# Part of an HBM-to-HBM quadrant swap sent through SBUF, beside direct copies

## The chip, the cores and the metric

The kernel runs on one core of one Trainium2 chip; the other cores have nothing to do. The metric is the device time of one execution in microseconds. The time before is the median of three runs. The profile is of one execution and gives a span a little shorter than the timed figure.

## What is computed

The input `x` is a matrix of 8192 x 8192 float32, which is 256 MiB or 268.44 MB. The output is `np.fft.ifftshift(x)`: as both sides are even, rows are rotated by 4096 and columns by 4096, so that the four quadrants change places diagonally.

```python
def setup_inputs():
    return {"x": np.random.randn(8192, 8192).astype(np.float32)}

def reference(x):
    return np.fft.ifftshift(x)
```

Nothing is computed on the values. Every byte is read once from HBM and written once to HBM, at another place. Sizes below are in MiB where they count blocks, and in MB (10^6 bytes) where they stand beside rates.

## The kernel before

The kernel copies from HBM to HBM and never touches the on-chip memory SBUF. The list `quads` holds the four quadrants as pairs of an output region and the input region that goes there. A loop over the quadrants cuts each into `nsplit = 4` blocks of 1024 rows, and for each block line 41 issues one copy, a DMA of 1024 rows of 4096 columns, 16 MiB. There are 16 such DMAs, all issued by the sync engine (SP) in one queue, one after the other. One row of a block is 16 KiB of contiguous memory; the next row of the same block lies 32 KiB further on, for reads and for writes.

A DMA is carried out by the core's 16 DMA engines together. Each takes a sixteenth of its rows, here 64 rows, and moves each row as one packet, so that the program makes 16 x 1024 = 16384 packets of 16 KiB. [...]

The layer in which the kernel is written (Tile) puts the waits in. It hands out eight completion semaphores in turn, one to each DMA in its order of issue. A DMA that takes a semaphore again waits, on the engine that issues it, until the DMA that had it before has landed completely. In this kernel the ninth DMA so waits for the first, and so on. No copy depends on the data of another.

Of the kernel before, what the change touches and what calls it, by code (L numbers as in the profile page):

```python
# [1 line left out]

# [4 lines left out]


@with_exitstack  # L10
def kernel(
    ctx: ExitStack,
    tc: tile.TileContext,
    x: bass.AP,
    out: bass.AP,
):
    nc = tc.nc

    R, C = x.shape
    hr = R // 2  # L20
    hc = C // 2

    quads = [
        ((0, hr), (0, hc), (hr, R), (hc, C)),
        ((0, hr), (hc, C), (hr, R), (0, hc)),
        ((hr, R), (0, hc), (0, hr), (hc, C)),
        ((hr, R), (hc, C), (0, hr), (0, hc)),
    ]

    engines = [nc.sync]  # L30
    nsplit = 4
    k = 0
    for (or0, or1), (oc0, oc1), (ir0, ir1), (ic0, ic1) in quads:
        rows = or1 - or0
        step = rows // nsplit
        for s in range(nsplit):
            a = s * step
            b = a + step
            eng = engines[k % len(engines)]
            k += 1  # L40
            eng.dma_start(
                out=out[or0 + a : or0 + b, oc0:oc1],
                in_=x[ir0 + a : ir0 + b, ic0:ic1],
            )


# [1 line left out]
_INS = ['x']  # L48
_OUTS = [((8192, 8192), 'float32')]


def kernel(**inputs):
    import numpy as _np
    import concourse.bacc as _bacc
    import concourse.tile as _tile
    from concourse import mybir as _mybir
    from concourse.bass_utils import run_bass_kernel_spmd as _run

    nc = _bacc.Bacc("TRN2", target_bir_lowering=False, num_devices=1)  # L59
    arrays, args = {}, []  # L60
    for name in _INS:
        a = _np.ascontiguousarray(inputs[name])
        if a.dtype.kind in "iu":
            a = a.astype(_np.int64)
        arrays[f"in_{name}_dram"] = a
        args.append(nc.dram_tensor(f"in_{name}_dram", a.shape, _mybir.dt.from_np(a.dtype), kind="ExternalInput").ap())
    for i, (shape, dtype) in enumerate(_OUTS):
        dt = _mybir.dt.from_np(_np.dtype(dtype))
        args.append(nc.dram_tensor(f"out_{i}_dram", shape, dt, kind="ExternalOutput").ap())
    with _tile.TileContext(nc) as tc:  # L70
        kernel(tc, *args)
    r = _run(nc, [arrays], core_ids=[0])
    got = tuple(r.results[0][f"out_{i}_dram"] for i in range(len(_OUTS)))
    return got[0]
```

## Time and profile before

| what | before |
| --- | --- |
| time, median of 3 runs | 823.21 us (820.71 to 828.84) |
| span of the profiled execution | 811.5 us |
| bytes moved by the DMA engines | 268.44 MB in 16640 packets |
| mean rate of the DMA engines | 331 GB/s |
| HBM traffic, read and written | 2 x 268.44 MB, 662 GB/s over the span |
| DMA issues | 16 of 16384 KB, median 158.0 us from issue to landing |
| compute engines | idle; 4 small memsets on GpSimd, 0.2 us |

The rate of the DMA engines counts a byte once when it passes an engine, where it is read and written. For a copy from HBM to HBM the HBM's own traffic is twice that. The 256 packets beyond the 16384 are the small ones that count up the semaphores, one for each DMA on each engine. Where the profile gives a DMA share, it is the mean share of time in which the 16 DMA engines have a packet in hand, not a share of their peak rate.

### The profile page before, as it was taken

To read this page: it belongs to the slowest core of one execution; us is meant where nothing else is said; L and a number is where in the kernel's file an instruction comes from. 1 tells how busy PE (TensorE), PEld (TensorE's weight loads), DVE (VectorE), ACT (ScalarE), POOL (GpSimd) and SP (SyncE) were. 2 spreads that over 40 slices of the span, in tenths; PEclk is the share of its full clock that TensorE was granted. 3 is DMA by queue.
4 is the path that set the end of the run, shared out by engine and by line. 5 is a ranking of instruction groups with operands and counts; after the bars stand their busy time and mean duration, and the time that the engine had idled before them with its cause. 6 is when DMAs were issued, how large, how long until landed. Compare 5 with 4: busy or idle time off the path is not lost. (4 is left out here: it accounts for less than half of the span.)

```text
span 811.5 us, 61 instructions
## 1 busy us (share of the span) xinstructions
POOL 0.2 (0%) x4
## 2 busy tenths in 40 slices
POOL 0000000000000000000000000000000000000000
DMA  9999999999999999999999999999999999999998
GB/s 298 328 328 333 312 337 332 326 334 329 332 334 329 329 329 334 331 331 334 338 340 333 332 334 339 334 333 337 338 333 337 334 333 338 332 334 341 328 339 287
DMA packets 16640, 268.44 MB, mean 331 GB/s; under 512 B 256, under 2 KB 256, under 8 KB 256
## 3 DMA queue, kind: packets, MB, share of 16 engines
q1 hardware_dynamic: 16640, 268.44, 99.3%
HBM read 268.44 MB, written 268.44 MB: 662 GB/s over the span
## 5 line engine op out<-in xcount | busy, mean ns | idle before, releaser
L59 POOL MEMSET const-bfloat16-1.0<- 128x1 bf16 x1 | 0.1, 102 | 0.0
L59 POOL MEMSET const-uint8-127<- 128x1 uint8 x1 | 0.1, 101 | 0.0
L59 POOL MEMSET const-float32-0.0<- 128x1 f32 x1 | 0.1, 99 | 0.2 <-issue 0.2
L59 POOL MEMSET const-float32-1.0<- 128x1 f32 x1 | 0.1, 98 | 0.0
## 6 DMA issues: line engine op xcount, KB each, us to landing
out_dram<-in_x_dram SPq DMA_DIRECT2D x16, 16384.0 KB, 158.0
```

The lines of the kernel that those rows point to most:

```text
L59: nc = _bacc.Bacc("TRN2", target_bir_lowering=False, num_devices=1)
```

## The change

The last 1280 output rows (40 MiB) no longer go straight from HBM to HBM. They go through SBUF in pieces of 128 rows by 2048 columns (1 MiB, 8 KiB in each of the 128 partitions): one DMA loads a piece into a tile, and another stores it from there. There are 20 tiles, each with a buffer of its own, and 40 pieces, so each tile is used twice (`CYCLES = 2`). Loads and stores are issued by the scalar engine (ACT), from a queue of its own.

The other 6912 rows (216 MiB) remain direct copies on the sync engine, but in 108 DMAs of 128 rows by 4096 columns (2 MiB) rather than 16 MiB each. In the text of the kernel one direct copy follows each load and each store, and the copies left over come at the end. A DMA of 128 rows gives each engine 8 rows[...].

The idea is to let loads and stores, each of which uses HBM in one direction alone, run beside copies that use it in both.

```diff
+P = 128
+TILES = 20
+CYCLES = 2
...
+    piece = hc // 2
+    pool = ctx.enter_context(tc.tile_pool(name="bounce", bufs=1))
...
+    def src(row):
+        return (row + hr) % R
+    through = [
+        (row, col)
+        for row in range(R - P * TILES * CYCLES // 4, R, P)
+        for col in range(0, C, piece)
+    ]
+    direct = [
+        (row, col) for row in range(0, R - P * TILES * CYCLES // 4, P) for col in (0, hc)
+    ]
+    tiles = [pool.tile([P, piece], x.dtype, name=f"t{k}") for k in range(TILES)]
-    engines = [nc.sync]
-    nsplit = 4
...
-            eng.dma_start(
-                out=out[or0 + a : or0 + b, oc0:oc1],
-                in_=x[ir0 + a : ir0 + b, ic0:ic1],
+    def copy():
+        if direct:
+            row, col = direct.pop(0)
+            nc.sync.dma_start(
+                out=out[row : row + P, col : col + hc],
+                in_=x[src(row) : src(row) + P, hc - col : 2 * hc - col],
             )
+    for c in range(CYCLES):
+        for k, t in enumerate(tiles):
+            row, col = through[c * TILES + k]
+            oc = (col + hc) % C
+            nc.scalar.dma_start(out=t[:], in_=x[src(row) : src(row) + P, oc : oc + piece])
+            copy()
+        for k, t in enumerate(tiles):
+            row, col = through[c * TILES + k]
+            nc.scalar.dma_start(out=out[row : row + P, col : col + piece], in_=t[:])
+            copy()
+    while direct:
+        copy()
```

More of the change, by code (lines that the diff above doesn't have):

```diff
@@ L21 @@
     hc = C // 2
[L23 to L27, printed above, removed]
-    ]
-    engines = [nc.sync]
-    nsplit = 4
[L32 to L41, printed above, removed]
-                out=out[or0 + a : or0 + b, oc0:oc1],
-                in_=x[ir0 + a : ir0 + b, ic0:ic1],
-            )
+    piece = hc // 2
[6 more added lines that the diff above has]
+        for col in range(0, C, piece)
+    ]
+    direct = [
[8 more added lines that the diff above has]
+                in_=x[src(row) : src(row) + P, hc - col : 2 * hc - col],
+            )
+    for c in range(CYCLES):
[10 more added lines that the diff above has]
+        copy()
 _INS = ['x']
```

## The prediction

> **What bounds the kernel now.** I read the page's DMA lines first, since no compute engine has work.
>
> ```profile
> span 811.5 us, 61 instructions
> ...
> GB/s 298 328 328 333 312 337 332 326 334 329 332 334 329 329 329 334 331 331 334 338 340 333 332 334 339 334 333 337 338 333 337 334 333 338 332 334 341 328 339 287
> ...
> q1 hardware_dynamic: 16640, 268.44, 99.3%
> HBM read 268.44 MB, written 268.44 MB: 662 GB/s over the span
> ```
>
> The 16 DMA engines hold a packet during 99.3% of the span, and the rate is flat: one stage from end to end, no gaps. A 16 KiB packet takes 16 x 811.5 us x 0.993 / 16384 = 0.787 us on average. That isn't an engine's best. In the trace's packet records 34% of these packets took 608 or 611 ns, the least that occurs (26.8 GB/s an engine, 429 for 16); the median is 731, the longest 2053. So packets wait for something all engines share.
>
> Next, the direct copies by line, for whether issue is the limit, and the windows at the end, where some engines have finished (columns: length, GpSimd busy, clock, DMA share, GB/s).
>
> ```profile
> L41 SPq DMA_DIRECT2D out_dram<-in_x_dram x16: 582/49353/95664, 0.7 to 652.6; - x16
> ...
> DMA to landing us min/median/max: 53.7/158.0/199.5
> ```
>
> ```profile
> 804.00:806.00 2.00, 0.00 (x0) 1.00 1.05 344
> 806.00:807.00 1.00, 0.00 (x0) 1.00 0.91 295
> 807.00:808.00 1.00, 0.00 (x0) 1.00 0.81 279
> 808.00:809.00 1.00, 0.00 (x0) 1.00 0.68 246
> 809.00:810.00 1.00, 0.00 (x0) 1.00 0.20 82
> ```
>
> The last DMA was issued at 652.6 us, 159 us before the end: the queue is always full and issue costs nothing. At the end, rate over busy share rises from 295/0.91 = 324 through 279/0.81 = 344 and 246/0.68 = 362 to 82/0.20 = 410 GB/s (narrow windows, so rough). Fewer engines run faster each: the shared limit is HBM at some 662 GB/s of reads plus writes, with the engines' own ceiling of 429 GB/s above it.
>
> **What the Trainium skill says.** "HBM Reference", Specifications (TRN2), gives about 716 GB/s for the HBM of a pair of cores; 662 is 92% of it, so the trace agrees that little is left. "Advanced Engine Details and Errata", DMA Bandwidth Details, gives 27.2 GB/s for an engine; the best packets' 26.8 agrees. "DMA: Bandwidth & Descriptors", Issuing engines are not separate DMA queues, says DMAs from different engines share the same 16 DMA engines and interleave; the trace before has one queue and can't show it. The same page's Latency and other measured facts bears on a rival below.
>
> **The change, part by part.**
>
> Bytes. HBM still reads and writes 268.44 MB each: no HBM work is saved. The DMA engines carry the 40 MiB twice, in 40 loads and 40 stores of 1 MiB: 226.5 MB direct + 83.9 MB = 310.4 MB, 16% more. What was the slack resource is charged.
>
> Order. The text of the kernel pairs one direct copy (2 MiB) with each load or store (1 MiB). The order as built doesn't: Tile orders them load, copy, load, again and again, then store, copy, store, so there are **two loads or stores for each direct copy**: 40 groups with 80 loads or stores and 40 copies, and 68 copies alone at the end. All share the eight semaphores, so each DMA waits on its issuing engine for the one eight places before it in this common order. The copies can't run ahead of the loads: the ratio of bytes is 1 to 1, whatever the engines' arbitration gives.
>
> Waits. Behind a waiting DMA stand the later ones of its queue. Eight in flight are about 5 loads or stores and 3 copies, 11 MiB; at 407 GB/s (below) that is some 28 us of work. At the end eight copies are 16 MiB, 50 us. A copy that waits leaves the ACT queue filled, so I cost these waits at nothing. A store stands at least 20 DMAs behind its load, and the load that reuses a tile as far behind the store: both are covered by the same waits. Issues cost at most some 0.6 us (the shortest on SP is 582 ns) for 188 DMAs on two engines in 800 us: hidden under transfers in flight. The tiles use no compute engine.
>
> Mixed part, 40 groups. In one group each engine moves 16 packets of 8 KiB (two loads or stores) and 8 of 16 KiB (one copy). An unobstructed 8 KiB packet takes 307 ns in the trace (three of the start-up transfers' packets; half of 611 is 305).
> - Lower end: 16 x 0.307 + 8 x 0.611 = 9.80 us, 40 groups 392 us. HBM then carries 6 MiB = 6.29 MB a group, 642 GB/s, just under 662.
> - Upper end: the copies' packets stay at 0.787: 16 x 0.307 + 8 x 0.787 = 11.21 us, 448 us.
> - What I take: while both queues hold packets, 8 copy packets and 8 small ones draw 5 MiB from HBM; at 662 GB/s that is 7.92 us. The other 8 small packets run alone at engine speed, 2.46 us. Together 10.38; the 16 engines are not in step, which fills some of HBM's slack, so **10.3 us a group, 412 us**, or 167.8 MB at 407 GB/s.
>
> The same data before (120 MiB net, 60 times 2 MiB) took 60 x 8 x 0.787 = 378 us. Even the lower end loses 14 us; my value loses 34.
>
> Last part: 68 copies x 8 packets x 0.787 us = 428 us, taking a copy of 2 MiB to run at the rate of one of 16 MiB.
>
> Edges: 811.5 - 16384/16 x 0.787 = 6 us for start and end, kept. From span to time: 823.21 - 811.5 = 11.7 us, kept.
>
> Sum: 412 + 428 + 6 = 846 us span, **858 us time, 4.2% slower**.
>
> **The rivals.**
> - Engine-bound, no HBM obstruction in the mix (the shared limit eases as soon as a third of the packets use it in one direction only): 392 + 428 + 6 + 11.7 = 838 us, 1.8% slower. For it: 642 is below 662. Against: it is so close that every packet at its minimum is unlikely, when 66% miss it now.
> - HBM no better beside loads: 448 + 428 + 6 + 11.7 = 894 us. Or one direction is the limit: then 20 groups run at 9.80 us and the other 20, where 4 MiB go that way at 331 GB/s, take 12.7 us, 449 us in all and 895. Against both: mixed HBM traffic would then fall to about 560 GB/s with the engines partly obstructed.
> - Faster: direct copies alone speed up with the new shape. The engines then work 256 KiB apart rather than 2 MiB, and some of the obstruction may be clashes of places in HBM. If packets alone fell from the mean 0.787 to the median 0.731, the last part would take 398 us, and with the mix at its floor 392 + 398 + 6 + 11.7 = 808 us, 1.9% faster. For it: packets range from 608 to 2053 ns. The skill's section named above lists copies that slow with large power-of-two row pitches: 207 of 214 GB/s at 512 KiB and 164 at 2 MiB. With 8 rows an engine I work that out as engines 4 and 16 MiB apart; at 2 MiB apart, as before, I estimate under 3% lost. Its full rate of 214 lies far below the 331 measured here, so it is weak evidence, and against this case.
> - No change: the same gain at about half the size, near 823.
>
> **How the numbers follow.** My case 0.50 (858); engine-bound 0.17 (838); HBM no better, or one direction, 0.15 (894); faster 0.10 (808); no change 0.08 (823). Slower by over 1%: 0.50 + 0.17 + 0.15 = 0.82. The range goes from 830, a little under the engine-bound case, to 896, over the two worst; out are faster, no change and a little above, about 0.2.
>
> **What would show each step right or wrong.** The page after should show 310.4 MB in about 27,000 packets (24,064 of data and 188 x 16 for semaphores), at a mean of 310.4/846 = 367 GB/s, with the HBM line near 635. By slices the rate should be about 407 for the first half, then fall to about 334. Windows: the mix ends near 415 us; 390 means engine-bound, 450 HBM no better. If the last 68 copies take under 413 us, the term for copies alone is wrong; if the rate dips between slices or the DMA share falls under 0.95 in the mix, the waits are not free. If the first part passes 429 GB/s, the engines' ceiling is wrong, and with it the whole argument.

## The result, and the profile after

The changed kernel took 860.07 us (median of 3 runs, 858.95 to 861.73) against 823.21 us: 1.043 times before, 95% interval 1.037 to 1.049. It is slower.

The page of the changed kernel, the lines that answer to those shown of before (the GB/s line gives the DMA engines' rate in 40 equal slices of the span; q1 is the sync engine's queue, q10 the scalar engine's):

```profile
span 858.3 us, 233 instructions
...
GB/s 364 378 405 401 410 409 414 413 411 412 389 413 414 392 403 418 411 407 415 378 341 319 323 327 324 325 319 328 321 322 318 320 328 321 318 325 328 328 320 252
DMA packets 27074, 310.41 MB, mean 362 GB/s; under 512 B 3008, under 2 KB 3008, under 8 KB 3008
...
q1 hardware_dynamic: 15552, 226.50, 74.7%
q10 hardware_dynamic: 11520, 83.89, 24.6%
...
HBM read 268.44 MB, written 268.44 MB: 626 GB/s over the span
```

The engines carry 310.41 MB rather than 268.44, and HBM's traffic, the same in bytes, runs at 626 GB/s rather than 662. So HBM is worked less hard than before, while q1 and q10 together still fill 99.3% of the 16 engines' time. The rate falls halfway, from some 410 to some 323 GB/s. The windows of the two parts (columns: length, GpSimd busy, clock, DMA share, GB/s):

```profile
20.00:420.00 400.00, 0.00 (x0) 1.00 1.01 406
460.00:850.00 390.00, 0.00 (x0) 1.00 0.99 323
```

In the second part there are direct copies alone: 323 GB/s through the engines is 646 at HBM, 2% under the 662 of before. In the first, each group of two loads or stores and one copy moves 4 MiB through the engines and 6 MiB at HBM: 406 is 609 GB/s at HBM, well under that limit, and close to the 429 of the engines. So the engines bind here for the most part. In the trace's packet records the 16 KiB packets in the first 420 us take 642 ns on average and the 8 KiB packets 329, against least times of 608 and 307.

Where did the time go? In the engines' time, one group took 16 x 0.329 + 8 x 0.642 = 10.4 us, and 40 of them 416 us. The same data as direct copies, 60 of 2 MiB at the 0.796 us a packet that the timed runs of before imply (working below), are 382 us. That is 34 of the 37 us lost.

The queue of the sync engine, by what it waited for (columns: who waited, for what; us in total, times, longest us). L49 is the line of the direct copy; `t<-in_x_dram` is a load, `out_dram<-t` a store:

```profile
SPq L49 <- DMA out_dram<-in_x_dram: 335.1, 57, 6.6
SPq L49 <- DMA t<-in_x_dram: 210.4, 20, 16.6
SPq L49 <- DMA out_dram<-t: 202.2, 22, 13.4
```

In the mix, direct copies were held back by loads for 210 us and by stores for 202 us. So the engines got two loads or stores to a copy: from 20 to 420 us they started 9742 packets of 8 KiB and 5040 of 16 KiB. No DMA engine stood idle for it (share 1.01), so these waits look free. They are not: they set which kind of bytes the engines had to hand, as the experiments show.

### The profile page after: what moved, and what is told of

It reads as the page before. It is cut to its first block, busy times and chain, and to the rows that moved or that the text cites. A ratio compares the mean times of both kernels' runs of the same rounds, so it can differ in the third digit from the quotient of the medians.

```text
span 858.3 us, 233 instructions
## 1 busy us (share of the span) xinstructions
POOL 0.2 (0%) x4
## 2 busy tenths in 40 slices
DMA packets 27074, 310.41 MB, mean 362 GB/s; under 512 B 3008, under 2 KB 3008, under 8 KB 3008
## 3 DMA queue, kind: packets, MB, share of 16 engines
HBM read 268.44 MB, written 268.44 MB: 626 GB/s over the span
```

## The experiments

My theory: bytes through SBUF pass the DMA engines twice; with two loads or stores to one copy the mix needs the engines (429 GB/s at best) more than it needs HBM (some 660), so slack moves to HBM and is lost. The order as built and the eight shared semaphores keep it at that ratio. The rivals: the shape of the smaller copies costs; a second queue costs; a fixed cost of entering and leaving the SBUF part; or every byte through SBUF costs the same whatever stands beside it.

Four runs were made on another chip: the one queue in the order as built, the change again, the thinner mix, and the loads and stores on semaphores of their own. Before took 814.5 us beside these four and 824 to 825 beside the other eight, so runs are compared by their ratio to before.

### Copies of 2 MiB alone

```diff
-    nsplit = 4
+    nsplit = 32
```

> All 256 MiB as 128 direct copies of 2 MiB on one queue, nothing through SBUF. If the smaller copies ([...]eight semaphores over 16 MiB) are what makes the copies alone take 0.804 us a packet in the changed kernel: 1024 packets an engine x 0.804 + 8 = 831 us span, 1% over before. If the shape costs nothing and the loss is all in the SBUF part: 823, as before.

824.67 us, ratio 1.000 (0.998 to 1.002). The shape of the direct copies costs nothing that shows. The profile of before, then that of this run, columns as above:

```profile
20.00:800.00 780.00, 0.00 (x0) 1.00 1.00 333
20.00:800.00 780.00, 0.00 (x0) 1.00 1.00 328
```

Copies alone differ by this much from one execution to another. The 323 GB/s in the changed kernel's profile is a little lower still; the same kernel, run again below, has 328 there.

### Two queues of direct copies

```diff
-    engines = [nc.sync]
+    engines = [nc.sync, nc.scalar]
```

> The kernel before, its 16 copies issued in turn from the sync and the scalar engine. If HBM's 662 GB/s is what bounds direct copies, a second queue changes nothing: 823 within 1%. If a queue's own packets in flight are the limit, two queues come near the engines' 429 GB/s: about 630 us. If switching between two queues costs, slower than 830.

822.82 us, ratio 0.996 (0.992 to 0.999). A second queue hardly lifts the limit, and it doesn't cost. What bounds direct copies lies behind the queues.

### Loads alone, then stores alone

```diff
-    for c in range(CYCLES):
...
+    pieces = [(row, col) for row in range(0, R // 2, P) for col in range(0, C, piece)]
+    for n, (row, col) in enumerate(pieces):
+        nc.scalar.dma_start(out=tiles[n % TILES][:], in_=...)
+    for n, (row, col) in enumerate(pieces):
+        nc.scalar.dma_start(out=out[row : row + P, col : col + piece], in_=tiles[n % TILES][:])
```

> No direct copies: 128 loads of 1 MiB into the 20 tiles, then 128 stores of 1 MiB from them, 134 MB each way (half of the matrix is left out, and the stores write what the tiles last held, so the output holds other rows). If the engines' ceiling is 26.8 GB/s each: 313 us a stage at 429 GB/s, 8 KiB packets at 307 ns. If one direction of HBM is limited to the 331 GB/s that direct copies show: 405 us a stage.

641.68 us (one run). The windows inside the loads and inside the stores, columns as above:

```profile
20.00:300.00 280.00, 0.00 (x0) 1.00 1.01 422
340.00:620.00 280.00, 0.00 (x0) 1.00 1.01 422
```

Either direction runs at 422 GB/s, close to the 429 worked out from the shortest packets, and well above the 331 that each direction has in direct copies. So the limit of direct copies is not one direction of HBM but the sum of both, and the engines' own ceiling stands at some 422. Whether that sum is bounded in the HBM itself or on the way to it, no run here tells apart.

### Half and twice the bytes through SBUF

```diff
-CYCLES = 2
+CYCLES = 1
```

> The change with one round instead of two: 20 MiB through SBUF, 118 direct copies. If each byte through SBUF is charged for its second passage of the DMA engines, half the bytes cost half: 20 groups x 10.4 us + 98 copies x 6.43 + 8 = 846 us span, about 848. If the cost is a fixed one (a second queue, start and end of the SBUF part), it stays near 860.

836.88 us, ratio 1.014 (1.008 to 1.019). The window of its copies alone:

```profile
260.00:820.00 560.00, 0.00 (x0) 1.00 1.00 331
```

```diff
-CYCLES = 2
+CYCLES = 4
```

> The change with four rounds: 80 MiB through SBUF, 88 direct copies. Charged by bytes: 80 groups x 10.4 us + 8 copies x 6.43 + 8 = 891 us span, about 893. A fixed cost: near 860. If stores and loads of neighbouring rounds blocked each other, over 910.

879.39 us, ratio 1.064 (1.060 to 1.068). With four rounds the mix lasts nearly to the end, and its window shows the rate of the changed kernel's first part again:

```profile
20.00:800.00 780.00, 0.00 (x0) 1.00 1.01 409
```

The loss grows with the bytes, so it is no fixed cost. Both losses are smaller than I expected: 12.5 us for 20 groups and 55 for 80, or 0.6 to 0.7 us a group, where the changed kernel loses 0.9 (0.8 when run again below). The time of copies alone may explain part of this: 331 GB/s in the one-round profile, 323 in that of the change. The loss per group is known no better than that.

### One queue, in the order of the text

```diff
-            nc.sync.dma_start(
+            tc.keep_in_program_order(nc.sync.dma_start(
...
-            nc.scalar.dma_start(out=t[:], in_=...)
+            tc.keep_in_program_order(nc.sync.dma_start(out=t[:], in_=...))
...
```

The stores are changed as the loads are. `keep_in_program_order` makes Tile keep a DMA where the text has it.

> The change's DMAs, all from the sync engine in the order of its text: one load or store, then one direct copy, so that bytes through SBUF and direct bytes stand 1 to 2 in the mix; 28 copies are left alone. If the mix of the change is bound by the engines because it has too few direct bytes beside the loads and stores, this one is bound by HBM again: a group (5 MiB of HBM traffic) takes 5.24 MB / 662 GB/s = 7.92 us, 80 groups 634, 28 copies x 6.43 = 180, with edges 8 and 2: 824 us, near before. If only the bytes through SBUF count, whatever stands beside them: near 860. If packets of one queue cannot overlap each other as those of two can: over 860.

834.32 us, ratio 1.009 (1.006 to 1.012). The same 40 MiB go through SBUF as in the change, but 80 copies stand beside them and not 40, and four fifths of the loss are gone. The window of its mix:

```profile
20.00:630.00 610.00, 0.00 (x0) 1.00 1.01 389
```

A group is now one load or store and one copy, 3 MiB through the engines and 5 at HBM: 389 is 648 GB/s at HBM. The engines have slack against their 422, HBM has next to none.

### One queue, in the order as built

```diff
-            copy()
+            if n % 2 == 0:
+                copy()
+            n += 1
```

> All from the sync engine, in the order that the changed kernel has as built: two loads or stores to one direct copy. It differs from the changed kernel in the number of queues alone, and from the run with one queue in text order in the ratio alone. If the ratio in the mix is what costs: as the changed kernel, about 855. If the second queue is what costs: about 834, as the run with one queue in text order.

842.64 us, ratio 1.034 (1.031 to 1.038). It differs from the run above in the ratio alone (this edit, after each load and each store), and from the changed kernel in the number of queues alone.

```profile
20.00:380.00 360.00, 0.00 (x0) 1.00 1.01 420
440.00:830.00 390.00, 0.00 (x0) 1.00 1.00 327
```

In its mix the engines reach 420 GB/s, their ceiling in loads and stores alone, and HBM stands at 420 x 1.5 = 630. The ratio makes most of the loss, with one queue as with two: 1.034 at two to one against 1.009 at one to one, with the same bytes through SBUF.

### The change again

The changed kernel without an edit, on the other chip.

> The changed kernel once more, beside the next three, so that all four stand against the same runs of before. Expected: 1.043 times before, about 860; if the first measurement lay high, 1.03, which would put it on the line through one round (1.0137) and four rounds (1.0642).

847.26 us, ratio 1.040 (1.037 to 1.043). It repeats, and does not come down to 1.03, where a line through one and four rounds passes; why is open.

```profile
span 845.3 us, 233 instructions
...
HBM read 268.44 MB, written 268.44 MB: 635 GB/s over the span
```

```profile
20.00:420.00 400.00, 0.00 (x0) 1.00 1.01 411
460.00:840.00 380.00, 0.00 (x0) 1.00 0.99 328
```

The single queue above is 0.6 points lower at the same ratio, and its mix ran at 420 GB/s where this one ran at 411. The two intervals overlap a little, so what the second queue adds is small and hardly clear of the noise.

### A thinner mix

```diff
-CYCLES = 2
+CYCLES = 1
...
             copy()
+            copy()
...
```

> All from the sync engine, one round (20 MiB through SBUF), two direct copies after each load or store. A group of one load or store and two copies draws 9 MiB from HBM, 9.44 MB / 656 GB/s = 14.4 us (656 is 537 MB over the 818 us that two queues took); an engine needs only 8 x 0.307 + 16 x 0.611 = 12.2 us. If HBM's sum of reads and writes bounds it, 40 groups 575, 38 copies x 6.38 = 242, edges 8 and 2: 827, at most 1% from before. If every byte through SBUF costs as in the change with one round: 837. If reads and writes mixed unevenly make HBM faster: under 815.

824.74 us, ratio 1.011 (1.008 to 1.015), with two copies after each load or store (the lines that put all on the sync engine in the order of the text are as above).

```profile
20.00:560.00 540.00, 0.00 (x0) 1.00 1.01 367
600.00:810.00 210.00, 0.00 (x0) 1.00 1.00 329
```

Five MiB through the engines are 9 at HBM: 367 is 661 GB/s, and copies alone are at 658. A mix with slack at the engines gets no more from HBM than copies get. I expected at most 1% over before, and it is about that. HBM's bytes are those of before, so what is lost is rate: the timed runs of before beside it imply, by an estimate, 536.9 MB / (814.5 - 1.8 - 6) us = 665 GB/s, where this run has 661 in the mix and 658 after it. Why both stretches run up to 1% lower stays open.

### Loads and stores on semaphores of their own

```diff
-            nc.scalar.dma_start(out=t[:], in_=...)
+            nc.gpsimd.dma_start(out=t[:], in_=...)
...
-            nc.scalar.dma_start(out=out[row : row + P, col : col + piece], in_=t[:])
+            nc.gpsimd.dma_start(out=out[row : row + P, col : col + piece], in_=t[:])
```

> The change with loads and stores issued by GpSimd instead of ACT. They then count on semaphores of their own, so that direct copies wait for direct copies alone, and may run ahead; the order as built is still two to one. If the shared semaphores hold the copies back to 1 to 1 in bytes: the queues now share the engines packet by packet, 16 KiB to 8 KiB, 80 copies go beside the 80 loads and stores, and the time is that of the one queue in text order, about 834. If the shared semaphores play no part: about 860. If GpSimd's way of issuing is itself a cost: over 870.

820.27 us, ratio 1.006 (1.004 to 1.009). The same DMAs, in the same order as built, lose 0.6% rather than 4.0%. In the changed kernel's trace eight completion semaphores count all 188 DMAs; here eight count the 108 copies and eight others the loads and stores. The waits of the sync engine's queue:

```profile
SPq L49 <- DMA out_dram<-in_x_dram: 707.9, 100, 8.3
```

Copies now wait for copies alone, and the lines for loads and stores are gone. The mix stretches to some 640 us:

```profile
20.00:640.00 620.00, 37.64 (x71) 1.00 1.01 398
680.00:800.00 120.00, 0.00 (x0) 1.00 1.00 333
```

398 GB/s at 5 to 3 is 663 at HBM, copies alone are at 666. The packet records show that it is 5 to 3: between 20 and 640 us the engines started 10013 packets of 8 KiB and 10040 of 16 KiB. The Trainium skill says under "DMA: Bandwidth & Descriptors", Queues, rings and completion order, that each engine takes its queues in turn, packet by packet. The equal counts agree with that. They don't show the turns themselves, and the page's packet may hold several pieces of memory, where the trace's packet is one row. Equal numbers of packets are two bytes of copy for one of load or store. In the changed kernel, where the copies had to wait, the counts were two to one. This run changes the way of issuing along with the semaphores, and lets 16 DMAs be in flight rather than eight, so for the semaphores it doesn't stand alone; the waits of the changed kernel's queue say the same. That the ratio costs is shown by the two runs on one queue, where it is the only edit.

### Where the engines work

I took each engine's share of a copy to be consecutive rows, so that in the kernel before the engines work 64 rows, or 2 MiB, apart. The packet records have neither engine nor address, so no run shows this. The first edit below deals the rows out in turn, the second makes the copies larger.

```diff
-                out=out[or0 + a : or0 + b, oc0:oc1],
-                in_=x[ir0 + a : ir0 + b, ic0:ic1],
+                out=out[or0 + a : or0 + b, oc0:oc1].rearrange("(j e) c -> e j c", e=16),
+                in_=x[ir0 + a : ir0 + b, ic0:ic1].rearrange("(j e) c -> e j c", e=16),
```

> The kernel before with the rows of a copy dealt out in turn[...]. If clashes of places in HBM make packets wait, the time moves by more than 1%, either way; if it is the sum of reads and writes alone, 823 within 1%.

825.3 us, ratio 0.999 (0.997 to 1.001).

```diff
-    nsplit = 4
+    nsplit = 1
```

> The kernel before with one copy of 4096 rows for each quadrant[...]. If clashes of places grow with the distance of the engines, slower than 830; if only the sum of reads and writes counts, 823 within 1%.

826.82 us, ratio 1.002 (1.000 to 1.004). With the kernel before and the copies of 2 MiB, rows have been dealt out in four ways. If my reading is right, the engines were 32 KiB, 256 KiB, 2 MiB and 8 MiB apart. No ratio moved by more than 0.2%, and the intervals reach to 0.4%.

## Why the prediction was right

It gave 858 us; 860.07 was measured. By its steps:

- **What bounds the kernel before**: HBM's sum of reads and writes with the engines' ceiling above it. Neither a second queue (0.996) nor another shape (0.999 to 1.002) moves it, one direction alone reaches 422 GB/s, and three mixes with slack at the engines stop at 648, 661 and 663 GB/s of the sum. That a sum of both directions binds is shown; that it is HBM's own is not.
- **The order as built and the shared semaphores** fix two loads or stores to one copy. The sync queue's waits and the packet counts show it, and the run in which the copies are let go agrees. The tie is not quite strict: some 44 copies rather than 40 had begun when the last store's packets landed at 437 us, so the end of the mix came later than the forecast sign of 415 us.
- **The waits cost nothing in themselves**: the DMA share is 1.01 in the mix, so this holds for idle engines. Their cost is the ratio that they impose, which the sum did contain; the step did not say that nearly all of the forecast loss hangs on it.
- **The mixed part**: 10.3 us a group was predicted, 10.4 measured; 412 against 416 us. It was inside its bounds, 9.80 and 11.21. How it splits was not foreseen: I had the small packets at their shortest, 0.307, and they took 0.329; the sum left (7.92 - 2.46) / 8 = 0.68 to a copy's packet, and it took 0.642. In a group that is 0.35 us too little and 0.32 too much, which cancel: that is luck.
- **Copies alone**: 428 us predicted. The packet records leave 435 for the 68 copies, 0.799 us a packet and not 0.787.
- **From span to time**: 11.7 us predicted, and this term was wrong: it took the lead of a quick execution for a cost beside the span. In the changed kernel's profiled run the difference is 860.07 - 858.3 = 1.8 us. The profiled execution of before, with its 811.5 us, was 10 us quicker than the timed ones. Taking off 1.8 and the edges of 6, the timed 823.21 us imply (823.21 - 1.8 - 6) / 1024 = 0.796 us a packet. So 0.787 was too short by 1%, and the 11.7 us made up for most of it. With 0.796 and 1.8 the sum had been 412 + 433 + 6 + 1.8 = 853 us. The close hit owes something to two errors that cancel. The parts themselves are borne out where executions are as quick as the profiled one: on the chip where before took 814.5 us, the changed kernel's packet records give 411 us for the groups and 427 for the 68 copies, in a span of 845.3, against 412, 428 and 846 predicted.
- **The rivals**: engine-bound with no obstruction at all (838) falls because the mix took 10.4 us a group and not 9.80: packets still stretch by 5 to 7%, even where the engines bind. HBM no better (894) falls with the copies' 642 ns. The faster case rested on clashes of places, of which the runs on shape show no sign.

What stays open: the last 0.6 to 1.1% that remain with slack at the engines, and where between engines and HBM the sum of both directions is bounded.

## What to carry to other kernels

Where a copy is bound by HBM's reads plus writes, a detour through SBUF saves no HBM byte and charges the DMA engines twice; here it was nearly free, at 0.6 to 1.1%, only while enough direct copies stood beside it to keep HBM full. Work out for each stage the bytes at each of the two limits, and not only the total. And look at the order as built and at what each DMA waits for: semaphores shared by two queues tie them to one pace, and that cost some 3% here, without one idle engine in the profile.

## What was not expected of the hardware

HBM's sum of reads and writes from one core stayed at 646 to 666 GB/s in all windows of copies alone shown here and in every mix with slack at the engines (648, 661, 663), whether reads and writes were even or 3 to 2: an uneven mix does not make HBM faster. And the size of the copies, from 2 to 64 MiB at a row pitch of 32 KiB, and the way in which their rows are dealt out made no difference above 0.2%.
